# A two-layer decoder trunk in split fp32: a second pair of blocks in seven products in each layer's second FFN, part loads in a list of their own, a new block order

## The chip, the core and the metric

The kernel runs on one core of one Trainium2 chip. The metric is the device time of one execution in microseconds (us). The kernel before takes 984.8 us, the median of three runs (982.86, 984.80, 985.94).

## The reference

A decoder trunk of two layers over 256 tokens of width 1024. Each layer is a half-step SwiGLU FFN, a mixer (layer 0: mLSTM, layer 1: dilated attention, both beside a memory cross-attention), and a second half-step SwiGLU FFN. Between the layers stands a K/V projection. The change concerns the second FFN:

```python
D_MODEL, SEQ, D_FF = 1024, 256, 2816
def swiglu(h, w_gate, w_up, w_down):
    return (jax.nn.silu(h @ w_gate) * (h @ w_up)) @ w_down
...
for layer in range(DEPTH):
    x = x + 0.5 * swiglu(rms_norm(x, ffn1_norm[layer]), ...)
    ...
    x = x + mix
    x = x + 0.5 * swiglu(rms_norm(x, ffn2_norm[layer]), ffn2_w_gate[layer], ffn2_w_up[layer], ffn2_w_down[layer])
```

## The kernel before

**Split fp32.** Every large product is made of three: each operand is split into a high half (`hi`, rounded to the matmul's reduced fp32 format) and the rest (`lo`), and `mm3` (L773) adds x_hi w_lo + x_hi w_hi + x_lo w_hi in PSUM. Weights come from HBM as units of 128 x 1024 (512 KB) into six raw buffers. ScalarE casts a unit to `hi`, VectorE subtracts to get `lo` (`emit_unit`, L631), into a ring of eight `hi` and eight `lo` tiles. Units go through the ring strictly in the order of one list, made by `_stream` (L100); a unit is freed when TensorE has used it.

**The FFN.** The 2816 hidden columns are 11 blocks of 256. For each block and each half of the tokens (t = 0, 1), `gu` (L1061) makes gate and up side by side: 8 chunks of the inner dimension x 3 matmuls of 128x128 by 512 columns, so 48 for a block in four units. `hidden_blocks` (L1026) applies SiLU and the product; `placed` (L1036) turns the result through DRAM (tiles `hb`, `hd`, `ht`) and splits it (`hhb`, `hlb`). `dn` (L1068) makes the down product: 24 matmuls for a block in two units, added in four PSUM banks (`acc`) over all blocks. Block 10 is made at the end, between the last down products.

**Seven products.** In each layer's second FFN one pair of gate/up blocks (5 and 6) is a product of 2x2 quarters (tokens halves by inner halves, inner halves by blocks) and is made with seven products instead of eight (`seventh`, L1130). A product is 4 chunks x 3 = 12 matmuls in two units (k = 0, 2). Its name in a plan is two digits: "45" is product 4 of the pair that begins at block 5. Its activations are differences of quarters, made once per FFN by `sums` (L1102): it adds hi and lo to full tiles `xs`, subtracts quarters (`xd`), and splits the differences (`th`, `tl`). It begins 16 us (layer 0) or 8 us (layer 1) of planned time after the activations are there, and yields 0.5 us after each step. The tiles `xs` lie in the places `pb0` and `pb2`.

Its weights are combinations of quarters, made in three pairs of tiles that are reused in place (`SLOTS`, `remade` L609): a for products 2 and 1, b for 5, 3, 6, c for 4 and 7. Tile a is loaded from quarter 0, b from quarter 3, c from quarter 2 with quarter 0 added by an accumulating DMA from GpSimd's queue. Once product 5's weights are split, VectorE subtracts b from a and GpSimd's queue adds quarter 1 to b; then a is added to b (for 6, once 3 is split) and subtracted from c (for 7, once 4 is split). The results are combined from PSUM on VectorE (`g`, `e`).

**What sets the order.** The program is emitted by a planner: `_Model` (L241) keeps a clock for each engine with a cost for each operation, and chains of steps are emitted when their planned time has come. The order of the blocks is written by hand in `PLANS` (L54): g is gate/up, d is down. Part loads stood in the list of units: `early` (L595) sent one on every third load, from 14 units ahead on, and one pair's parts could be loaded only after the pair before was done (`may_load`, L707). Tile b is loaded only after `sums` (`summed`).

Of the kernel before, what the change touches and what calls it, by code (L numbers as in the profile page):

```python
# [8 lines left out]
F32 = mybir.dt.float32  # L9
# [3 lines left out]
ALU = mybir.AluOpType  # L13
# [40 lines left out]
PLANS = {(1, 2): "g0 g1 g2 d0 g3 d1 g4 d2 25 55 45 35 d3 15 65 d4 75 g7 g8 d5 d6 g9 d7", (0, 2): "g0 g1 g2 d0 g3 d1 g4 25 55 d2 45 35 d3 15 65 d4 75 g7 g8 d5 d6 g9 d7"}  # L54
# [6 lines left out]
EVERY = 3  # L61
# [3 lines left out]

SLOTS = {2: ("a", (0,), None), 5: ("b", (3,), None), 4: ("c", (2, 0), None),
# [174 lines left out]
class _Model:  # L241
# [71 lines left out]
    def product(self, columns, cycles, rows, outs, ins):  # L313
# [9 lines left out]
        self.run("tensor", cycles / (2400 if self.fast else 1200) + 0.0027, outs, ins)  # L323

    def run(self, engine, cost, outs, ins, delay=0.0):
# [8 lines left out]
        for a in outs:  # L334
            self.mark(a, end, True, engine)
        self.latest = max(self.latest, end)


class _Engine:
# [5 lines left out]
    def __getattr__(self, method):  # L345
        call, model, name = getattr(self.engine, method), self.model, self.name

        def traced(out, *args, **kw):
# [8 lines left out]
            if name == "sync" or name == "gpsimd" and method == "dma_start":  # L357
                model.run("sync", max(n * out.partition_size() * 4 / 360e3, 0.06), outs, ins, 2.0)
                return
# [50 lines left out]
class _Kernel:  # L410
    def __init__(self, tc, ctx, io, out, units):
# [18 lines left out]
        self.stored, self.slots, self.made, self.open, self.partp = {}, {}, {}, None, None  # L430
        self.todo, self.turn = [], 0
# [123 lines left out]
    def load_unit(self):  # L555
        i, self.loaded = self.loaded, self.loaded + 1
        if self.units[i][1] is None:
            return
        width = self.units[i][2]
        if self.units[i][1][0] == "parts":  # L560
            self.load_part(i)
            return
# [7 lines left out]
    def load_part(self, i):  # L570
        key = self.units[i][0]
        if self.open != key[1:4]:
            self.begin_parts(key[1:4])
        slot = SLOTS[key[4]][0], key[5]
        while slot not in self.slots:
            self.next_part()
        self.raw[i] = self.slots[slot]

    def begin_parts(self, pair):
        self.open = pair  # L580
        self.slots = {}
        self.todo = [(m, k) for m, k in ((4, 0), (2, 0), (4, 2), (2, 2), (5, 0), (5, 2))]

    def next_part(self):

        m, k = self.todo.pop(0)
        slot, parts, _ = SLOTS[m]
        t = self.work.tile([P, 1024], F32, tag="mem", name="pa") if slot == "a" else \
            self.partp[1].tile([P, 1024], F32, tag=f"p{slot}{k}", name=f"p{slot}{k}")
        self.slots[slot, k] = t  # L590
        self.nc.sync.dma_start(t, self.part_of(self.open + (parts[0], k)))
        for p in parts[1:]:
# [1383 lines left out]
```

## Time and profile before

| | us |
|---|---|
| median of three runs | 984.8 (982.86 to 985.94) |
| span of the profiled execution (first to last instruction) | 981.7 |
| second FFN of layer 0, from its first matmul to the K/V projection's | 319.4 to 499.4 |
| second FFN of layer 1, from its first matmul to the end | 798.3 to 981.7 |

PE is TensorE's matmuls, PEld its weight loads, DVE VectorE, ACT ScalarE, POOL GpSimd, SP SyncE (which issues nearly all DMAs). A row of a group gives the line, engine, operation, what is written and read with shapes, the count, then busy us and mean ns of one, then the idle time before and what ended it. In the chain in order of time a row is start, length, engine, tile, line, count. Most operations are recorded by one helper (L349), so the tile's name tells them apart. A matmul's own duration (about 390 ns) overlaps with its neighbours'; the step from one to the next is what counts. The granted clock of TensorE is 1.000 over the span.

### The profile page before, as it was taken

The numbers are of one execution on the slowest core, as the hardware profiler recorded it, in microseconds if no ns is written. First come the engines' busy times: TensorE is split into PE (matmuls) and PEld (weight loads), VectorE is DVE, ScalarE is ACT, GpSimd is POOL, SyncE is SP. The second block draws the span as 40 slices with busy tenths as digits, with TensorE's granted clock in tenths as the row PEclk, the third lists the DMA queues.
The fourth block names the chain that finished last, engine by engine and source line by source line (L and its number), as shares of the span: only waits on it lengthen the run. The fifth ranks groups of instructions, "written<-read, shape, count | busy, mean of one in ns | idle before, by whom it ended". The sixth has DMA issues, their size and how long they took to land.

```text
span 981.7 us, 13154 instructions
## 1 busy us (share of the span) xinstructions
PE 973.7 (99%) x4655; PEld 809.8 (82%) x4655; DVE 691.0 (70%) x1035; ACT 563.8 (57%) x903; POOL 52.2 (5%) x86
## 2 busy tenths in 40 slices
PE   9999999999999999999999999999999999999998
PEld 6888888899998888888878888888887788878887
DVE  5856656569886787976586677776576679589653
ACT  7656445477565655655466566565564585465541
POOL 0002000010010000000011000000002000000000
PEclk9999999999999999999999999999999999999999
DMA  9968677346355697388657688889627557945751
GB/s 353 321 212 302 212 239 227 112 148 230 118 193 193 202 318 243 116 290 268 235 179 252 226 318 274 336 301 316 246 86 266 207 175 252 375 99 205 272 166 43
DMA packets 85482, 223.95 MB, mean 228 GB/s; under 512 B 8172, under 2 KB 29608, under 8 KB 85416
## 3 DMA queue, kind: packets, MB, share of 16 engines
q1 hardware_dynamic: 84120, 218.88, 64.5%
q0 software_dynamic: 1152, 4.19, 2.3%
q8 instruction: 36, 0.59, 0.3%
q14 instruction: 30, 0.25, 0.1%
q10 hardware_dynamic: 144, 0.04, 0.0%
HBM read 203.66 MB, written 19.42 MB: 227 GB/s over the span
## 4 chain that ended last, share of the span: by engine, by line
PE 95%; DVE 2%; ACT 1%; DMA 1%; issue 1%; SPq 0%; DVEq 0%; ACTq 0%
PE gups L763 47%; PE acc L763 24%; PE aps L763 8%; PE oacc L763 4%; PE kvps L763 3%; PE bqps L763 2%; PE mkvps L763 2%; PE tps L770 1%; DVE s L349 1%; PE po L763 1%; PE tpp L770 1%; PE sc L763 1%; DMA ht<-hd 0%; PE ms L763 0%; PE pn L763 0%
## 5 line engine op out<-in xcount | busy, mean ns | idle before, releaser
L349 DVE TENSOR_TENSOR lo<-raw,hi 128x1024 fp32r<-128x1024 f32 (+2 forms) x263 | 302.7, 1167 | 85.2 <-ACT hi L349 79.7
L349 ACT CAST hi<-raw 128x1024 fp32r<-128x1024 f32 (+2 forms) x263 | 260.1, 1008 | 95.3 <-PE acc L763 40.9
L763 PE MATMUL gups<-lo,xh 128*128 128x512 f32 x656 | 254.9, 391 | 1.6 <-DVE g L349 1.6
L763 PE MATMUL gups<-hi,xh 128*128 128x512 f32 x656 | 254.6, 390 | 0.4 <-ACT hi L349 0.4
L763 PE MATMUL gups<-hi,xl 128*128 128x512 f32 x656 | 254.4, 390 | 0.0
L763 PEld LDWEIGHTS gups<-lo,xh 128*128 128x128 f32 x656 | 123.2, 188 | 27.3 <-DVE g L349 2.1
L763 PEld LDWEIGHTS gups<-hi,xh 128*128 128x128 f32 x656 | 123.3, 188 | 26.4 <-ACT hi L349 1.3
L763 PEld LDWEIGHTS gups<-hi,xl 128*128 128x128 f32 x656 | 123.4, 188 | 26.0
L349 ACT ACTIVATE sil<-gups,rstd 128x256 f32<-128x256 f32 x84 | 39.7, 474 | 146.4 <-PE gups L763 136.3
L763 PE MATMUL acc<-lo,hhb 128*128 128x512 f32 x304 | 119.5, 393 | 0.0
L763 PE MATMUL acc<-hi,hlb 128*128 128x512 f32 x304 | 118.6, 390 | 0.1
L763 PE MATMUL acc<-hi,hhb 128*128 128x512 f32 x304 | 118.3, 389 | 0.0
L349 DVE SCALAR_TENSOR_TENSOR lo<-raw,gains,hi 128x512 fp32r<-128x512 f32 x144 | 99.6, 744 | 16.4 <-ACT hi L349 16.1
L349 DVE SCALAR_TENSOR_TENSOR h<-gups,rstd,sil 128x256 f32<-128x256 f32 x84 | 40.0, 480 | 91.1 <-ACT sil L349 91.0
L349 ACT ACTIVATE hi<-raw,gains 128x512 fp32r<-128x512 f32 x144 | 93.9, 715 | 14.9 <-PE gups L763 5.8
L763 PEld LDWEIGHTS acc<-hi,hlb 128*128 128x128 f32 x304 | 57.1, 188 | 12.4 <-DVE hlb L349 0.5
L763 PEld LDWEIGHTS acc<-lo,hhb 128*128 128x128 f32 x304 | 57.1, 188 | 11.6 <-ACT hhb L349 0.3
L763 PEld LDWEIGHTS acc<-hi,hhb 128*128 128x128 f32 x304 | 57.1, 188 | 11.4
L763 PE MATMUL aps<-lo,xh 128*128 128x384 f32 (+1 forms) x144 | 49.8, 346 | 0.0
L763 PE MATMUL aps<-hi,xl 128*128 128x384 f32 (+1 forms) x144 | 47.5, 330 | 0.0
L763 PE MATMUL aps<-hi,xh 128*128 128x384 f32 (+1 forms) x144 | 47.4, 329 | 0.0
L349 ACT CAST hhb<-ht 128x512 fp32r<-128x512 f32 x38 | 23.5, 619 | 26.4 <-DMA ht<-hd 26.3
(228 smaller groups left out, 1191.2 us busy)
## 6 DMA issues: line engine op xcount, KB each, us to landing
raw<-in_wts SPq DMA_DIRECT2D x294, 512.0 KB, 5.1
raw<-in_wts SPq DMA_DIRECT2D x32, 384.0 KB, 3.8
hd<-hb SPq DMA_DIRECT2D x38, 256.0 KB, 5.6
ht<-hd SPq DMA_DIRECT2D x38, 256.0 KB, 4.6
wo<-hi SPq DMA_DIRECT2D x8, 512.0 KB, 6.7
wo<-lo SPq DMA_DIRECT2D x8, 512.0 KB, 7.3
hi<-wo SPq DMA_DIRECT2D x8, 512.0 KB, 5.5
lo<-wo SPq DMA_DIRECT2D x8, 512.0 KB, 7.2
```

The source lines that it names most:

```text
L349: call(out, *args, **kw)
L763: self.pe.matmul(out, lhsT=lhsT, rhs=rhs, start=start, stop=stop, skip_group_check=more)
L770: self.pe.transpose(out, in_, ident)
```

## The change

Blocks 7 and 8 become a second pair ("27 57 ... 77") in both second FFNs, and both get the same order. The seven activations serve both pairs. A list `todo` of part loads in the order a, b, c for each pair replaces the turn-taking: a part is loaded when its pair's first unit is at most 14 units ahead, when the last product that uses the tile's old content has been split (`LAST`), for b when `summed` is set, and when the planned DMA queue is less than `LEAD` = 3 us ahead. The second pair's tile a has buffers of its own. The planner's cost of a matmul in fp32 at full clock gets 13.3 ns beside its columns instead of 2.7, and accumulating DMAs a cost of their own. The hidden operands `hh`, `hl` of ordinary blocks and some tiles of the mixers move from a shared pool of five buffers to pools of their own (two or four, and four or five buffers).

```diff
-PLANS = {(1, 2): "g0 g1 g2 d0 g3 d1 g4 d2 25 55 45 35 d3 15 65 d4 75 g7 g8 d5 d6 g9 d7", (0, 2): "g0 g1 g2 d0 g3 d1 g4 25 55 d2 45 35 d3 15 65 d4 75 g7 g8 d5 d6 g9 d7"}
+PLANS = {
+    (0, 2): "g0 g1 g2 g3 25 55 d0 d1 d2 45 35 15 65 75 "
+            "d3 g9 g4 27 57 d5 47 37 17 67 77 d4 d9 d6",
+    (1, 2): "g0 g1 g2 g3 25 55 d0 d1 d2 45 35 15 65 75 "
+            "d3 g9 g4 27 57 d5 47 37 17 67 77 d4 d9 d6",
+}
-EVERY = 3
+LEAD = 3.0
 EARLIER = 14
+PARTS = ((2, 0), (2, 2), (5, 0), (5, 2), (4, 0), (4, 2))
+LAST = {"a": (1, 3, 4), "b": (6,), "c": (7,)}
...
-        self.run("tensor", cycles / (2400 if self.fast else 1200) + 0.0027, outs, ins)
+        gap = 0.0133 if self.fast and ins[0].dtype == F32R else 0.0027
+        self.run("tensor", cycles / (2400 if self.fast else 1200) + gap, outs, ins)
...
+    def adding(self, cost, outs, ins):
+
+        start = max([self.clock["sync"]] + [self.ready(a, True, "sync") for a in outs])
+        self.clock["sync"] += cost
+        end = start + cost + 3.0
+        for a in outs:
+            self.mark(a, end, True, "sync")
+        self.latest = max(self.latest, end)
...
+    def begin_parts(self, layer, which, plan, pool):
+
+        self.partp, self.slots = pool, {}
+        self.pairs = [(layer, which, s[1]) for s in plan if s[0] == "st" and s[2] == 2]
+        self.todo = [(p, m, k) for p in range(len(self.pairs)) for m, k in PARTS]
+
+    def before_part(self):
+
+        p, m, k = self.todo[0]
+        slot = SLOTS[m][0]
+        p -= 2 if slot == "a" else 1
+        return [] if p < 0 else [(self.pairs[p], i, k) for i in LAST[slot]]
+
+    def part_ready(self):
+
+        if not self.todo:
+            return False
+        p, m, _ = self.todo[0]
+        if self.index[("st",) + self.pairs[p] + (2, 0)] > self.next + EARLIER:
+            return False
+        if SLOTS[m][0] == "b" and not self.summed:
+            return False
+        chains = [self.made.get(c) for c in self.before_part()]
+        return all(c is not None and c.done for c in chains)
...
     def next_part(self):
 
-        m, k = self.todo.pop(0)
+        p, m, k = self.todo.pop(0)
         slot, parts, _ = SLOTS[m]
-        t = self.work.tile([P, 1024], F32, tag="mem", name="pa") if slot == "a" else \
-            self.partp[1].tile([P, 1024], F32, tag=f"p{slot}{k}", name=f"p{slot}{k}")
...
+        if slot == "a" and p % 2 == 0:
+            t = self.work.tile([P, 1024], F32, tag="mem", name="pa")
+        else:
+            t = self.partp.tile([P, 1024], F32, tag=f"p{slot}{k}", name=f"p{slot}{k}")
...
+        while self.part_ready() and self.model.clock["sync"] < self.now + LEAD:
+            self.next_part()
...
-                hh = self.work.tile([P, FB], F32R, tag="hh", bufs=5, name="hh")
-                hl = self.work.tile([P, FB], F32R, tag="hl", bufs=5, name="hl")
+                hh = fp.tile([P, FB], F32R, tag="hs", bufs=few, name="hh")
+                hl = fp.tile([P, FB], F32R, tag="ls", bufs=few, name="hl")
...
-                    e = self.work.tile([P, 384], F32, tag="hh", bufs=5, name="e")
+                    e = mp.tile([P, 384], F32, tag="hh", bufs=4, name="e")
```

More of the change, by code (lines that the diff above doesn't have):

```diff
@@ L595, in early @@
-    def early(self):
-        for i in range(self.loaded, min(self.next + EARLIER, len(self.units))):
-            key, src = self.units[i][:2]
-            if src and src[0] == "parts" and self.open is None and self.may_load(i):
-                self.begin_parts(key[1:4])
-        self.turn += 1
-        if self.todo and (self.todo[0][0] != 5 or self.summed) and self.turn % EVERY == 0:
-            self.next_part()
+        if slot == "a" and p % 2 == 0:
+            t = self.work.tile([P, 1024], F32, tag="mem", name="pa")
+        else:
+            t = self.partp.tile([P, 1024], F32, tag=f"p{slot}{k}", name=f"p{slot}{k}")
@@ L605, in part_of @@
+        pair = self.pairs[p]
+        self.slots[pair, slot, k] = t
+        self.nc.sync.dma_start(t, self.part_of(pair + (parts[0], k)))
+        for i in parts[1:]:
+            self.nc.gpsimd.dma_start(t, self.part_of(pair + (i, k)), accum_op=ALU.add)
     def part_of(self, part):
@@ L611, in remade @@
         nc = self.nc
-        a, b, c = (self.slots.get((n, k)) for n in "abc")
+        a, b, c = (self.slots.get((pair, n, k)) for n in "abc")
         if m == 5:
@@ L682, in emit_unit @@
             self.load_unit()
+        if src is not None and src[0] == "parts":
+            slot = key[1:4], SLOTS[key[4]][0], key[5]
+            while slot not in self.slots:
+                self.finish(*[self.made[c] for c in self.before_part()])
+                self.next_part()
+            self.raw[i] = self.slots[slot]
         if src is None:
@@ L998, in ffn_in @@
         pairs = (layer, which) in PLANS
+        few = 4 if (layer, which) == (0, 1) else 2
         def activated(ps, t, out, last=False):
@@ L1077, in dn @@
             groups = [(slice(h * 512, (h + 1) * 512), acc[t][h], b == 0, last) for h in range(2)]
-            if (layer, which, t) == (1, 2, 1) and b >= NB - 2:
+            if (layer, which, t) == (1, 2, 1) and b in (left[1], NB - 1):
                 f, a, begins, _ = groups.pop()
@@ L1217, in ffn_in @@
         seven, gain = {}, folded(("gu", layer, which))
+        plan, left = _plan(layer, which)
         self.summed = False
@@ L1222, in ffn_in @@
             chains["sums"] = self.spawn(sums())
-            self.partp = (layer, which), fp
-        plan, left = _plan(layer, which)
+            self.begin_parts(layer, which, plan, fp)
         for step in plan:
```

61 lines of the change are left out of this document (17 added, 44 removed).

## The prediction

> **What bounds the kernel now.** I read the page first (busy shares, then the chain that ended last), then the chain in order of time around both second FFNs, then what TensorE waited for there.
>
> ```profile
> span 981.7 us, 13154 instructions
> PE 973.7 (99%) x4655; PEld 809.8 (82%) x4655; DVE 691.0 (70%) x1035; ACT 563.8 (57%) x903; POOL 52.2 (5%) x86
> ...
> PE 95%; DVE 2%; ACT 1%; DMA 1%; issue 1%; SPq 0%; DVEq 0%; ACTq 0%
> ```
>
> TensorE carries 95% of the chain, so the count of matmuls is the time. How much one costs is read from the chain in order of time, not from the mean duration of a matmul (matmuls overlap):
>
> ```profile
> 319.69 2.09 PE gups L763 x9
> 322.21 26.57 PE gups L763 x117
> ...
> 418.64 24.48 PE gups L763 x108
> 443.12 10.88 PE acc L763 x48
> ...
> 798.53 2.09 PE gups L763 x9
> 801.05 30.63 PE gups L763 x135
> ```
>
> 24.48 us over 108 matmuls and 10.88 over 48 are both 0.2267 us each: 512 columns without a hole. So a gate/up block (48) takes 10.88 us, a down block (24) 5.44, one product of a pair (12) 2.72. The first second FFN (layer 0) begins at 319.4, the other at 798.3. The holes in them are few; what the weight loads of TensorE waited for, and the two matmuls around the longest hole in the timeline:
>
> ```profile
> PEld gups L763 <- DVE g L349: 2.1, 1, 2.1
> PEld acc L763 <- DVE hlb L349: 0.5, 1, 0.5
> PEld acc L763 <- ACT hhb L349: 0.3, 1, 0.3
> ```
>
> ```profile
> 877.54 0.39 PE L763 MATMUL gups<-hi,xl 128*128 128x512 f32 x1
> 879.56 0.50 PE L763 MATMUL gups<-lo,xh 128*128 128x512 f32 x1 [1.64 <-DVE g L349]
> ```
>
> The one hole in layer 1's pair is 2.02 us from start to start, less 0.23 for the matmul in it: 1.8 lost. In layer 0 a down block's operand was late for 0.5 + 0.3 = 0.8.
>
> **The change, part by part.**
>
> *Removed: one product in eight of a second pair, in each layer.* Two ordinary gate/up blocks are 96 matmuls, a pair of seven products is 84. 12 x 0.2267 = 2.72 us per layer, 5.44 in all. Down blocks stay.
>
> *Removed: the two old holes.* Layer 1 ran products 2, 5, 4, 3 without a break, and 3 waited for a chain that begins at 5 (subtract, accumulating DMA, add, split). The new order has three down blocks (16.3 us) between 5 and 4 in the first pair and one (5.44) in the second, as layer 0 had before, where this place had no hole. The first down block now comes after product 5 and not beside the sums of activations, so its operand is in time. Together 1.8 + 0.8 = 2.6 us. What is late next is priced below.
>
> *Added: VectorE and ScalarE work.* A pair splits 14 weight tiles where two blocks split 8, remakes six tiles in place, and makes six combinations from PSUM. The windows of the two stages and of the old pair in layer 0, then the timeline and the groups of layer 0:
>
> ```profile
> core 0: us, PE busy (x) PEld busy (x) DVE busy (x) ACT busy (x) POOL busy (x), PEclk, DMA share, GB/s
> 319.50:499.40 179.90, 179.84 (x803) 148.29 (x802) 135.62 (x172) 101.61 (x138) 5.42 (x8) 1.00 0.71 233
> 798.50:981.70 183.20, 178.22 (x795) 147.20 (x793) 127.71 (x162) 89.97 (x119) 4.41 (x6) 1.00 0.60 204
> ...
> 386.00:421.40 35.40, 35.40 (x158) 29.31 (x157) 34.21 (x39) 22.73 (x26) 0.00 (x0) 1.00 0.47 157
> ```
>
> ```profile
> 400.86 0.68 DVE L349 TENSOR_TENSOR e<-gups,g 128x512 f32<-128x512 f32 x1
> 401.46 2.35 DVE L349 TENSOR_TENSOR lo<-pa,hi 128x1024 fp32r<-128x1024 f32 x2
> 403.73 2.35 DVE L349 TENSOR_TENSOR lo<-pb,hi 128x1024 fp32r<-128x1024 f32 x2
> ```
>
> ```profile
> L349 DVE TENSOR_TENSOR lo<-raw,hi 128x1024 fp32r<-128x1024 f32 x54 | 65.2, 1218 | 15.1 <-ACT hi L349 13.9
> L349 ACT CAST hi<-raw 128x1024 fp32r<-128x1024 f32 x53 | 55.1, 1051 | 18.0 <-PE gups L763 8.5 <-PE acc L763 7.4 <-DMA wo<-hi 1.0
> ```
>
> Queued, a 1024-wide VectorE step follows the last by 1.14 us (2.27 for two) and a 512-wide one by 0.60. Added per layer: 6 splits and 6 remakes at 1.14 and 6 combinations at 0.60, 17.3 us. VectorE was busy for 135.6 of 179.9 us in layer 0 and 127.7 of 183.2 in layer 1, so 153 and 145 of about 177: it still fits. ScalarE gets 6 casts of 1.05, which its 78 idle us of layer 0 cover. What matters is where VectorE's work stands. The old 386 to 421.4 is the old first pair with its three down blocks, 19.0 + 16.3 us of TensorE; VectorE was 34.2 of 35.4 us busy and TensorE had no hole. The new first pair has the same blocks, only with five products in one run at its end. Counted from product 5, VectorE owes 17 splits and 6 remakes (26.2), four combinations (2.4) and about 3.5 of activations and operands before the pair's last weight is due, 32.1 in all; TensorE covers 2.7 + 16.3 + 13.6 less the last 0.7, 31.9. That is level, so I put 1.0 there in layer 0, where VectorE starts with no lead, and 0 in layer 1. The second pairs follow a down block and two gate/up blocks (27.2 us of TensorE for some 19 of VectorE); I put 0.3 each. Bounds for all four pairs: 0, and a hole as in layer 1 before, 1.8 each.
>
> *Moved: the pairs come earlier, behind the sums.* Product 5 reads tiles that share their place with the sums of activations, so its load waits for the last use of those. Before the first pair there now stand four gate/up blocks, 192 matmuls; 41.0 us of them lie behind 322.21 and 801.05 (181 matmuls), so product 2 begins at 363.2 and 842.1 and product 5 at 366.0 and 844.8. In layer 0 that is 22 us earlier than before. The timelines of VectorE and SyncE there, and the landing of part b's loads in layer 0 (362 to 368) and in layer 1 (835 to 846):
>
> ```profile
> 346.80 0.69 DVE L349 TENSOR_TENSOR xd<-xs 128x512 f32<-128x512 f32 x1
> ...
> 348.84 0.65 DVE L349 TENSOR_TENSOR tl<-xd,th 128x512 fp32r<-128x512 f32 x1
> ...
> 362.65 0.68 DVE L349 TENSOR_TENSOR xd<-xs 128x512 f32<-128x512 f32 x1
> ...
> 363.36 0.81 SPq L349 DMA_DIRECT2D pb<-in_wts  x2
> ...
> 816.32 0.68 DVE L349 TENSOR_TENSOR xd<-xs 128x512 f32<-128x512 f32 x1
> ...
> 838.17 1.80 SPq L349 DMA_DIRECT2D pb<-in_wts  x2
> ```
>
> ```profile
> pb<-in_wts SPq DMA_DIRECT2D x2, 512.0 KB, 3.6
> ```
>
> ```profile
> pb<-in_wts SPq DMA_DIRECT2D x2, 512.0 KB, 9.3
> ```
>
> Five differences are taken of the sums. The first took 2.7 us from its start to the end of its low half; with the code's pause of 0.5 that is 3.2 apart if nothing comes between, so the last could end 4 x 3.2 + 0.7 after 346.8, at 360.3; before, among weight splits, it let the load go at 363.36. In the new order fewer splits stand there: weights are split in order, eight ahead at most, and the split of product 5 itself stops those behind it. I take 361.8. The landing took 3.6 in layer 0, with the queue quiet, and 9.3 in layer 1, with other part loads beside it; now loads of part a go early and those of c behind b, so I take 3.6. With the cast (1.05) and the split (1.22) the weights are there at 367.7: a wait of 1.7 us in layer 0. Ends: 0.2, and 363.4 + 9.3 + 2.3 - 366.0 = 9.0. In layer 1 the same count from 816.3 gives 829.8, and even 9.3 + 2.3 behind it is 841.4, ahead of 844.8: 0. Its other end is the old issue, 838.2 + 11.6 - 844.8 = 5.0. Behind a late split everything of ScalarE and VectorE queues that was issued later, the down blocks' weights first; they have 16 us before they are missed.
>
> *DMAs.* Per layer SP issues two loads fewer and GpSimd four accumulating ones more, 1.05 MB in all. The page's list of DMA issues, then the full list's row of the accumulations into b:
>
> ```profile
> hd<-hb SPq DMA_DIRECT2D x38, 256.0 KB, 5.6
> ht<-hd SPq DMA_DIRECT2D x38, 256.0 KB, 4.6
> ```
>
> ```profile
> pb<-in_wts POOLq DMA_DIRECT2D x4, 512.0 KB, 7.1
> ```
>
> Averaged over the stages (the windows above) the queues were 0.71 and 0.60 busy, so the bytes cost nothing. An accumulation (7.1) lies under 19.0 us (three down blocks and product 4) in the first pair and 8.2 plus VectorE's lead in the second; if that lead is gone, about 2 us a pair, inside the bound above. GpSimd has no other work there but the statistics at a stage's start. At the end, product 7 of the last pair needs the way through memory, 5.6 + 4.6, and the operand's split; 21.8 us (three down blocks and half of the last gate/up block) hide it: nothing.
>
> *The planner's clock and buffers.* The planner now counts 226.7 ns for a matmul where it counted 216, which is the pitch measured above. It reorders the emission everywhere, in the mixers too, where most of the 3% of the chain that is VectorE's and ScalarE's lies (29 us). A tenth of it either way, 3 us, is my bound; I take 0. Own buffers for hidden operands and mixer tiles: 0, a wait there would need five live at once.
>
> *Sum.* -5.44 - 2.6 + 1.7 + 1.0 + 4 x 0 + 2 x 0.3 = -4.7. Against the profiled span, 981.7 becomes 977.0. The median of the runs is 984.8, 3.1 above the span, and I leave that alone: 980.1, rounded to **980.0 us**.
>
> **Rivals.** *A: VectorE becomes the bound inside pairs.* Each of four pairs loses what one lost before, 1.8 to 2 us, and the 1.7 in layer 0 stays: 984.8 - 8.0 + 7.6 + 1.7 = 986 at worst, about 984.5 with half of the old holes. For it: 34.2 of 35.4 us busy already, and 17 us more per layer. Against it: that very window had no hole.
>
> *B: slower, by the late part.* If the sums end as before and the load lands as late as in layer 1, product 5 waits 9.0 and 5.0: -8.0 + 14.0 + 1.6 = +7.6, 992.4. It decides from a total wait at product 5 of 9.4 us (8.0 - 1.6 + 3.0). For it: the pair comes 22 us earlier and nothing hurries the sums. Against it: the load queue is emptier then. A long wait may cost more than itself:
>
> ```profile
> 1.25 4.02 PE L1867 MATMUL warm<-warm 128*128 128x512 bf16 x9 [1.25 <-DVE warm L349]
> ```
>
> Out of idleness the first nine matmuls took 0.45 each, twice the pitch; the 2.02 us hole left the next ones at 0.23. If a wait of 9.0 brought that state back for such a 4 us, half of it, 2.0 us, comes on top: 994.4; I give this extra a chance of 0.03 within B. The Trainium skill has it as a rule ("TensorE: Matmul & The Clock Gate", Part 1: an idle window of about 3.4 us halves the clock until a busy window has passed); by it 1.7 us would come on top of every wait above 3.4. The trace agrees at the start and, with 2.02 us, does not reach the limit.
>
> *C: all is covered.* Only the gains stay: 984.8 - 8.0 = 976.8.
>
> **How the numbers follow.** Forecast (978 to 982) 0.48, A 0.25, B 0.13, C 0.14. The range of 8 in 10 reaches from C with a little of the planner's bound, 975.5, to the worst of A, 986.0. What this measurement can tell from no change is about 0.3%, 3 us: faster is below 981.8, slower above 987.8. Faster gets C and nearly all of the forecast, 0.60; same gets A and the forecast's edge, 0.25; slower B and a little of A, 0.15.
>
> **What would show it.** TensorE has 24 matmuls fewer; both FFNs still run at 0.2267. The hole at layer 1's product 3 is gone. In layer 0 a hole of 1 to 3 us stands ahead of product 5, with the load of part b or its cast named as the one waited for. VectorE's busy time rises by about 35 us. I am wrong if the holes in the two FFNs together exceed 8 us, or if the mixers change by more than 3 us.

## The result: slower by 2.2%, and the profile after

The kernel after takes **1005.65 us** (median of four runs, 1004.26 to 1008.73). The kernel before took 983.83 beside it (982.81 to 985.94), so the ratio is 1.0225 (95% interval 1.0202 to 1.0249). The forecast was 980.0, with 986.0 as the upper end. The profiled execution of the new kernel took 1008.73; its span is 1007.0, where 977.0 was expected. So 30.0 us have to be found. That execution is the slowest of the four, 3.1 above their median, so the sizes below are its own and a little large.

First the page of the new kernel: span, busy time, and the chain that ended last by engine.

```profile
span 1007.0 us, 13163 instructions
...
PE 978.6 (97%) x4631; PEld 809.6 (80%) x4631; DVE 725.6 (72%) x1071; ACT 577.8 (57%) x917; POOL 60.7 (6%) x94
...
PE 62%; DMA 15%; DVE 14%; issue 4%; ACT 4%; SPq 0%; POOL 0%; ACTq 0%; DVEq 0%; POOLq 0%
```

The work is what was forecast: 4631 matmuls, 24 fewer, and 34.6 us more of VectorE (35 were expected). What changed is the chain: 15% of it is now DMA (1% before) and 14% VectorE. A third of it now runs through transfers, VectorE and ScalarE, where TensorE carried 95% before.

Where the 30.0 us lie is read from the first matmuls of the stages:

| us | before | forecast | after | off by |
|---|---|---|---|---|
| second FFN, layer 0 | 179.8 | 179.3 | 190.8 | 11.5 |
| second FFN, layer 1, to the end | 183.4 | 179.2 | 189.4 | 10.2 |
| all the rest | 618.5 | 618.5 | 626.8 | 8.3 |

The forecast columns are the prediction's own terms: -2.72 - 0.8 + 1.7 + 1.0 + 0.3 in layer 0, -2.72 - 1.8 + 0.3 in layer 1. The old hole at layer 1's product 3 is gone, as forecast. The rest consists of first FFNs, mixers and the K/V projection, of which the change edits nothing but buffers and the planner's clock.

What TensorE waited for, the two longest entries of the list of waits:

```profile
PE gups L780 <- DVE h L366: 14.2, 4, 6.1
PE gups L780 <- DVE g L366: 1.7, 1, 1.7
```

The columns are total, count and longest, in us. `h` is the product of gate and up of an ordinary block, VectorE's last read of its PSUM bank. Four waits for it make 14.2 us: one ahead of each product 5, in both pairs of both layers. Here is the worst, TensorE's timeline in the second pair of layer 0:

```profile
435.76 0.39 PE L780 MATMUL gups<-hi,xl 128*128 128x512 f32 x1
...
438.48 0.39 PE L780 MATMUL gups<-hi,tl 128*128 128x512 f32 x1
444.92 0.80 PE L780 MATMUL gups<-lo,th 128*128 128x512 f32 x1 [6.05 <-DVE h L366]
445.51 0.63 PE L780 MATMUL gups<-hi,th 128*128 128x512 f32 x1
445.94 0.63 PE L780 MATMUL gups<-hi,tl 128*128 128x512 f32 x1
```

Product 2 ends, and product 5 begins 6.44 us later instead of 0.23: 6.2 lost. Its weights are not late. It needs a bank: gate and up of a block use two banks in turn, product 2 takes the one of t = 0, and product 5 the one of t = 1, which is free only when ScalarE's SiLU and then `h` have read it. The last matmul of that half starts at 435.76 (the first line), so SiLU could run from 436.2. The timelines of ScalarE and of VectorE show when it did:

```profile
440.52 0.62 ACT L366 CAST hhb<-ht 128x512 fp32r<-128x512 f32 x1 [9.26 <-DMA ht<-hd]
441.04 1.99 ACT L366 CAST hi<-raw 128x1024 fp32r<-128x1024 f32 x2
442.93 0.47 ACT L366 ACTIVATE sil<-gups,rstd 128x256 f32<-128x256 f32 x1
```

```profile
433.03 0.68 DVE L366 TENSOR_TENSOR hlb<-ht,hhb 128x512 fp32r<-128x512 f32 x1
...
442.13 2.34 DVE L366 TENSOR_TENSOR lo<-raw,hi 128x1024 fp32r<-128x1024 f32 x2
444.39 0.48 DVE L366 SCALAR_TENSOR_TENSOR h<-gups,rstd,sil 128x256 f32<-128x256 f32 x1
```

ScalarE stood for 9.26 us at `hhb`, the cast of a down block's turned operand, because the transfer that makes `ht` had not landed. Two casts of weights and the SiLU followed it in the queue and ran only after it, and VectorE's splits and `h` after those. SiLU ran 6.8 us after its data were there. And why was `ht` late? SyncE's timeline:

```profile
425.01 9.11 SPq L366 DMA_DIRECT2D ht<-hd  x2
```

These are two loads into the one buffer that `ht` has: the second is issued at 434, since the split of the block before (`hlb` at 433.03 above) had to release the buffer first. That split itself ran 2.2 us after its cast, behind weights of the pair in VectorE's queue.

Layer 1's second pair, ScalarE, then VectorE:

```profile
929.02 0.62 ACT L366 CAST hhb<-ht 128x512 fp32r<-128x512 f32 x1 [5.84 <-DMA ht<-hd]
...
932.75 0.47 ACT L366 ACTIVATE sil<-gups,rstd 128x256 f32<-128x256 f32 x1
```

```profile
933.40 1.22 DVE L366 TENSOR_TENSOR lo<-pc,hi 128x1024 fp32r<-128x1024 f32 x1
934.65 1.23 DVE L366 TENSOR_TENSOR pc<-pc,pa 128x1024 f32<-128x1024 f32 x1
935.79 0.48 DVE L366 SCALAR_TENSOR_TENSOR h<-gups,rstd,sil 128x256 f32<-128x256 f32 x1
```

Such a cast waited 5.84 us here, half a block earlier. The SiLU ended at 933.2, and `h` came 2.6 us later, behind a split and a remaking of the pair's weights.

In the first pairs the same bank is late behind other instructions. Layer 0, ScalarE, then VectorE:

```profile
369.07 1.05 ACT L366 CAST hi<-pb 128x1024 fp32r<-128x1024 f32 x1 [2.28 <-DMA pb<-in_wts]
370.03 0.46 ACT L366 ACTIVATE sil<-gups,rstd 128x256 f32<-128x256 f32 x1
```

```profile
370.16 1.22 DVE L366 TENSOR_TENSOR lo<-pb,hi 128x1024 fp32r<-128x1024 f32 x1 [2.23 <-ACT hi L366]
371.30 1.22 DVE L366 TENSOR_TENSOR pa<-pa,pb 128x1024 f32<-128x1024 f32 x1
372.43 0.48 DVE L366 SCALAR_TENSOR_TENSOR h<-gups,rstd,sil 128x256 f32<-128x256 f32 x1
372.83 1.22 DVE L366 TENSOR_TENSOR lo<-pb,hi 128x1024 fp32r<-128x1024 f32 x1
```

Layer 1, ScalarE, then VectorE:

```profile
861.65 1.05 ACT L366 CAST hi<-pb 128x1024 fp32r<-128x1024 f32 x1 [0.77 <-DMA pb<-in_wts]
862.60 2.00 ACT L366 CAST hi<-raw 128x1024 fp32r<-128x1024 f32 x2
864.50 0.47 ACT L366 ACTIVATE sil<-gups,rstd 128x256 f32<-128x256 f32 x1
```

```profile
863.18 1.22 DVE L366 TENSOR_TENSOR lo<-pb,hi 128x1024 fp32r<-128x1024 f32 x1
864.32 1.22 DVE L366 TENSOR_TENSOR pa<-pa,pb 128x1024 f32<-128x1024 f32 x1
865.46 2.35 DVE L366 TENSOR_TENSOR lo<-raw,hi 128x1024 fp32r<-128x1024 f32 x2
867.73 0.48 DVE L366 SCALAR_TENSOR_TENSOR h<-gups,rstd,sil 128x256 f32<-128x256 f32 x1
```

Part b is loaded late because of the sums, as the prediction said; but its casts also hold the SiLU back, and then the remaking of `pa` holds `h` back. The weights themselves come in two halves (the rows `lo<-pb`). In layer 0 the second was there at 374.05, and without any wait it would have been needed at 372.2: the late weights alone would have lost 1.8. In layer 1 it was there at 864.4, when product 5 could only have begun: there the bank alone was late. Lost ahead of product 5, start to start less 0.23: 2.1 and 6.2 in layer 0, 3.85 and 2.65 in layer 1. Single holes of 0.8 to 1.9 besides (product 7 behind `g` at 403.8, operands of down blocks) bring the holes to about 11.4 and 7.7.

After two of them TensorE also ran slower. The windows from 444 to 456 and from 860 to 875 (columns as in the prediction):

```profile
444.00:456.00 12.00, 11.08 (x37) 8.96 (x38) 11.90 (x14) 7.85 (x10) 0.00 (x0) 0.72 0.44 135
860.00:875.00 15.00, 11.31 (x39) 8.74 (x38) 12.85 (x14) 11.07 (x13) 3.59 (x4) 0.77 0.95 242
```

The granted clock is 0.72 and 0.77 there. Twelve matmuls behind 444.92 follow each other by 0.43 instead of 0.2267: 12 x 0.2 = 2.4 us lost, and as much in layer 1.

Last, the 8.3 us outside. The waits of ScalarE for turned operands, before and then after, show that something has moved everywhere:

```profile
ACT hhb L349 <- DMA ht<-hd: 26.3, 19, 4.2
```

```profile
ACT hhb L366 <- DMA ht<-hd: 58.7, 26, 9.3
```

### The profile page after: what moved, and what is told of

It is laid out like the page before. It is cut to its first block, busy times and chain, and to the rows that moved or that the text cites. A ratio compares the mean times of both kernels' runs of the same rounds, so it can differ in the third digit from the quotient of the medians.

```text
span 1007.0 us, 13163 instructions
## 1 busy us (share of the span) xinstructions
PE 978.6 (97%) x4631; PEld 809.6 (80%) x4631; DVE 725.6 (72%) x1071; ACT 577.8 (57%) x917; POOL 60.7 (6%) x94
## 4 chain that ended last, share of the span: by engine, by line
PE 62%; DMA 15%; DVE 14%; issue 4%; ACT 4%; SPq 0%; POOL 0%; ACTq 0%; DVEq 0%; POOLq 0%
PE gups L780 24%; PE acc L780 17%; DVE lo L366 7%; PE aps L780 6%; DMA hd<-hb 6%; DMA ht<-hd 5%; PE oacc L780 4%; PE kvps L780 3%; PE bqps L780 2%; DMA pb<-in_wts 2%; ACT hi L366 2%; DMA wo<-hi 1%; PE tps L787 1%; DVE h L366 1%; PE mkvps L780 1%
## 5 line engine op out<-in xcount | busy, mean ns | idle before, releaser
L366 DVE TENSOR_TENSOR lo<-raw,hi 128x1024 fp32r<-128x1024 f32 (+3 forms) x247 | 282.9, 1162 | 79.9 <-ACT hi L366 75.2
L366 ACT CAST hi<-raw 128x1024 fp32r<-128x1024 f32 (+3 forms) x247 | 242.8, 1006 | 92.6 <-PE acc L780 33.5
L780 PE MATMUL gups<-hi,xh 128*128 128x512 f32 x608 | 236.3, 391 | 0.7 <-ACT hi L366 0.7
L780 PE MATMUL gups<-lo,xh 128*128 128x512 f32 x608 | 236.6, 392 | 0.0
L780 PE MATMUL gups<-hi,xl 128*128 128x512 f32 x608 | 236.3, 391 | 0.0
L780 PEld LDWEIGHTS gups<-hi,xh 128*128 128x128 f32 x608 | 114.6, 189 | 25.2 <-ACT hi L366 1.6
L780 PEld LDWEIGHTS gups<-hi,xl 128*128 128x128 f32 x608 | 114.7, 189 | 24.0
L780 PEld LDWEIGHTS gups<-lo,xh 128*128 128x128 f32 x608 | 114.6, 188 | 23.6
L780 PEld LDWEIGHTS acc<-hi,hhb 128*128 128x128 f32 x304 | 57.4, 189 | 11.4
L366 ACT CAST hhb<-ht 128x512 fp32r<-128x512 f32 x38 | 23.6, 620 | 58.7 <-DMA ht<-hd 58.7
L366 DVE TENSOR_TENSOR hlb<-ht,hhb 128x512 fp32r<-128x512 f32 x38 | 26.1, 688 | 35.1 <-ACT hhb L366 35.0
L780 PE MATMUL gups<-lo,th 128*128 128x512 f32 x80 | 33.8, 422 | 15.9 <-DVE h L366 14.2
```

The source lines that it names most:

```text
L366: call(out, *args, **kw)
L780: self.pe.matmul(out, lhsT=lhsT, rhs=rhs, start=start, stop=stop, skip_group_check=more)
```

## The experiments

Four theories stood against each other. **Clock**: the planner's truer cost of a matmul emits steps that wait for transfers too early. **Queue**: a step that waits for a DMA stands in ScalarE's queue ahead of the SiLU that frees product 5's bank. **Order**: the new order itself leaves too little between the blocks. **VectorE**: it simply has too much to do in the pairs (the prediction's rival A). Each ratio is against the kernel before on the same chip, with its 95% interval. Sums "outside" and of the FFNs are spans of the stages as in the table above. They come from the one profiled execution of each run, which can lie 3 to 6 us from the run's median (e3, e13, e15), so differences of 1 or 2 us between them prove little.

### e1: the clock alone, in the kernel before

```diff
-        self.run("tensor", cycles / (2400 if self.fast else 1200) + 0.0027, outs, ins)
+        gap = 0.0133 if self.fast and ins[0].dtype == F32R else 0.0027
+        self.run("tensor", cycles / (2400 if self.fast else 1200) + gap, outs, ins)
```

> The kernel before, with one line changed: the planner counts 226.7 ns for a fast matmul instead of 216. Theory 'planner's clock': the 8.4 us that the changed kernel lost outside the two second FFNs (first FFN 2.7, mixers 2.0 and 1.9, the others 1.8) come from this line, so the run takes 990 to 993 us. Rival 'own buffers' (the hidden operands and mixer tiles that moved to pools of their own cause them): the run stays at 984, within 1.5 us.

996.71 us (995.55 to 998.58), ratio 1.0129 (1.0109 to 1.0149): over half of the loss with one number and no second pair. Outside 626.5 (+8.0, as after the whole change), layer 0's second FFN 183.9 (+4.1), layer 1's unchanged. Most of the 4.1 is seen at product 5. ScalarE's timeline before:

```profile
384.28 0.62 ACT L349 CAST hhb<-ht 128x512 fp32r<-128x512 f32 x1
384.80 1.05 ACT L349 CAST hi<-pc 128x1024 fp32r<-128x1024 f32 x1
386.04 0.47 ACT L349 ACTIVATE sil<-gups,rstd 128x256 f32<-128x256 f32 x1 [0.19 <-PE gups L763]
```

and in e1:

```profile
391.24 0.62 ACT L350 CAST hhb<-ht 128x512 fp32r<-128x512 f32 x1 [2.75 <-DMA ht<-hd]
391.77 1.05 ACT L350 CAST hi<-pc 128x1024 fp32r<-128x1024 f32 x1
392.72 0.46 ACT L350 ACTIVATE sil<-gups,rstd 128x256 f32<-128x256 f32 x1
```

The same three instructions. Before, the transfer had landed, and SiLU waited for the matmuls alone. In e1 the cast waits 2.75 us, and TensorE stands 3.33 us from start to start. The old kernel had this place as well, and little room in it: TensorE's and VectorE's timelines there are

```profile
388.56 0.39 PE L763 MATMUL gups<-lo,th 128*128 128x512 f32 x1
```

```profile
387.29 0.48 DVE L349 SCALAR_TENSOR_TENSOR h<-gups,rstd,sil 128x256 f32<-128x256 f32 x1
```

so `h` had released the bank at 387.8, 0.8 us before product 5.

### e2: the whole change with the old clock

```diff
-        gap = 0.0133 if self.fast and ins[0].dtype == F32R else 0.0027
-        self.run("tensor", cycles / (2400 if self.fast else 1200) + gap, outs, ins)
+        self.run("tensor", cycles / (2400 if self.fast else 1200) + 0.0027, outs, ins)
```

> The changed kernel, with that one line put back to 216 ns. Theory 'planner's clock': the stages outside the second FFNs return to their old lengths and the run takes about 997 us; the holes ahead of product 5 stay, since they do not come from it. Rival 'own buffers': 1005, as it was. If the planner's clock also makes the holes in the second FFNs, the run comes near 984 or below it.

1012.74 (1010.54 to 1014.49), ratio 1.0289 (1.0266 to 1.0312). Outside it is back to 619.6, so all but 1.1 of the 8.3 us there are the clock's. But both second FFNs are longer than with the new clock (198.6 and 194.6): there the truer clock helps. The clock can't be the only cause.

### e3: the turned operand's cast emitted 4 us later

```diff
             nc.sync.dma_start(ht, bass.AP(d.tensor, d.offset, [[P, P], [32 * 512, 4], [1, P]]))
-            yield
+            yield 4.0
```

> The changed kernel, with the cast of a turned hidden operand emitted 4 us later in planned time (the pause after its load is 4.0 instead of 0). Theory 'head of the queue': in layer 0's second pair ScalarE stood 9.3 us at such a cast whose load had not landed, the SiLU that frees product 5's PSUM bank stood behind it, and TensorE lost 6.2 us and then 2.7 at half clock; with the cast later these 8.9 go and most of the 2.65 of layer 1's second pair, and the run takes 994 to 998. Rival 'VectorE's throughput' (17 us more VectorE work per layer is what holds TensorE): 1005, within 2.

1002.54 (998.43 to 1007.99), ratio 1.019 (1.0149 to 1.023). ScalarE's wait for `ht` falls from 58.7 to 6.9, and the hole of 6.44 in layer 0's second pair to 2.5; the FFNs win 3.9 and 3.2. The queue theory holds for that hole. Layer 1's second pair keeps one of 3.06, where such a cast still waits 2.48, and the time lies between the two expectations. The profiled run is the fastest of a wide range, so these sizes are rough.

### e4: the new order and clock, with one pair

```diff
-            "d3 g9 g4 27 57 d5 47 37 17 67 77 d4 d9 d6",
+            "d3 g9 g4 g7 d5 g8 d4 d9 d6",
```

> The changed kernel with blocks 7 and 8 as ordinary blocks again in the place of the second pair, one pair in seven products per layer as before, in the new order. Theory 'head of the queue': the holes of the first pairs stay (2.1 + 0.8 in layer 0, 3.85 and 2.7 of half clock in layer 1), those of the second pairs go (6.2 + 2.7 + 1.9 and 2.65), 5.4 us of products come back: about 998. Rival 'VectorE's throughput': with 17 us less for it in each layer no hole is left in the second FFNs, about 990.

1004.81 (999.73 to 1006.89), ratio 1.0201 (1.0161 to 1.024). Without a second pair the time is nearly that of the full change. First-pair holes stay, 4.43 and 3.86 from start to start. The FFNs are 186.5 and 187.3, shorter by 4.3 and 2.1 although 2.72 of products came back in each: the second pair brought 7.0 and 4.8 of losses, and the rest is there without it. So VectorE's load from two pairs can't be what makes the first pairs' holes; for the second pairs this run doesn't decide it.

### e5: a down block between products 2 and 5

```diff
-    (0, 2): "g0 g1 g2 g3 25 55 d0 d1 d2 45 35 15 65 75 "
-            "d3 g9 g4 27 57 d5 47 37 17 67 77 d4 d9 d6",
+    (0, 2): "g0 g1 g2 g3 25 d0 55 d1 d2 45 35 15 65 75 "
+            "d3 g9 g4 27 d5 57 d4 47 37 17 67 77 d9 d6",
```

(and the same for layer 1).

> The changed kernel with another order: a down block stands between products 2 and 5 of each pair (25 d0 55 d1 d2 45 ... and 27 d5 57 d4 47 ...), so that the PSUM bank of the last gate/up block has 8.2 us instead of 2.7 to be freed. Theory 'bank': the four holes ahead of product 5 (2.1, 6.2, 3.85 and 2.65 with twice 2.7 at half clock) shrink by 5.4 us each, all but 1 us of the 20 goes, about 987; where the accumulation into b has only product 4 to cover it in the second pair, 1 to 3 us come back: 987 to 991. Rival 'VectorE's throughput': the holes stay, 1003 to 1006.

1030.7 (1027.78 to 1033.55), ratio 1.0478 (1.0453 to 1.0503), the worst of all. The bank is no longer waited for, but the list of waits has a new head:

```profile
PE acc L780 <- ACT hhb L366: 19.2, 4, 8.5
```

I had moved block 4's down product close behind the block itself, and its way through memory was not done: holes of 5.83 and 8.88. This order was a bad test of the bank; it shows only that the other side of the same resource, the turned operand, is as tight.

### e6 and e8: e1 with landings planned longer, or the cast later

```diff
-                model.run("sync", max(n * out.partition_size() * 4 / 360e3, 0.06), outs, ins, 2.0)
+                model.run("sync", max(n * out.partition_size() * 4 / 360e3, 0.06), outs, ins, 4.0)
```

> The kernel before with the planner at 226.7 ns per matmul and with 4.0 instead of 2.0 us planned for a load or a store to land. Theory 'planned landing': the true clock costs 12 us only because ScalarE then gets casts of turned operands too early against a landing that is planned at 2.7 and takes 4 to 7; with 4.0 the waits of ScalarE on those (60.6 us, 26.3 in the kernel before) fall below 30 and the run comes back to 982 to 987. Rival 'detuned' (any change of the planner's clock spoils an order that was fitted to the old one): 992 or more.

e8 has the edit of e3 in its place:

> The kernel before with the planner at 226.7 ns per matmul and with only the casts of turned hidden operands emitted 4 us later in planned time. Theory 'planned landing': it is these casts that stand at the head of ScalarE's queue, so most of the 12 us goes: 984 to 989. If other waits matter as much (weight loads, the accumulations), 990 to 996.

e6: 999.55 (998.98 to 999.76), ratio 1.016 (1.0145 to 1.0176). Layer 0's first FFN and mixer are back to 199.6 and 119.8, and the wait for `ht` is down to 10.3; outside, 4.3 of the 8.0 are won. The time misses the expected 982 to 987 all the same, for TensorE now waits for operands that come late:

```profile
PE acc L764 <- ACT hhb L350: 8.3, 3, 5.1
```

e8: 993.74 (992.62 to 994.1), ratio 1.01 (1.0085 to 1.0115). Layer 0's hole at product 5 is gone, and ScalarE's wait for `ht` is 9.7. But holes of 2.22 and 1.23 behind late operands take its place, so that layer 0's FFN stays at 184.1, and outside it stays at 624.8. So the cast at the head of the queue explains the hole in the FFN, and not the loss in the mixers: that one reacts to the planned landing of all loads, and only in part.

### e7 and e9: the same two edits in the kernel after

e7 is the kernel after with a planned landing of 4.0, as in e6:

> The changed kernel with 4.0 instead of 2.0 us planned for a load or a store to land. Theory 'planned landing': the 8 us outside the second FFNs and the parts of the holes that come from casts standing at the head of ScalarE's queue go, 985 to 992. Rival 'detuned': 1000 or more.

1000.46 (998.2 to 1002.19), ratio 1.017 (1.0146 to 1.0193). Outside 621.4, 5.4 better than after; holes at the second pairs' product 5 remain, 5.14 and 3.51. e9 is e7 with the edit of e3 on top:

> The changed kernel with 4.0 us planned for a landing and the cast of a turned hidden operand another 4.0 us later in planned time. With the first alone, ScalarE still stood 4.6 us (layer 0) and 2.9 us (layer 1) at such a cast ahead of the SiLU that frees product 5's bank in the second pairs, and TensorE lost 4.9 and 3.3 there. Theory 'head of the queue': both holes go, 990 to 993. Rival: something else holds that SiLU, and the run stays at 1000.

1018.31 (1017.06 to 1020.41), ratio 1.0349 (1.0326 to 1.0372). A miss: both of those holes go, and others come, behind down operands that are cast too late (9.0 for `hhb`, 3.8 for `hlb` in the list of waits); the rest grows to 630.1. Two remedies for the same wait overshoot.

### e10: two buffers for the turned operand

```diff
-            ht = fp.tile([P, 4, P], F32, tag="ht", bufs=1, name="ht")
+            ht = fp.tile([P, 4, P], F32, tag="ht", bufs=2, name="ht")
```

> The changed kernel with two buffers instead of one for the turned hidden operand (ht). In front of the second pair four blocks (5, 6, 9, 4) go through memory one after the other, since the load of the next waits until the one before has been split. Theory 'single buffer': with two, the landings keep pace, the 9.3 us that ScalarE stood in layer 0 shrink to under 4, the hole ahead of product 5 there goes below 3 with no half clock, about 997. Rival: the round trip itself is too long for the plan, and the run stays within 3 us of 1005.

1000.45 (999.92 to 1002.9), ratio 1.017 (1.0148 to 1.0193). The holes at product 5 are gone in both second pairs, with no change of order or clock; those of the first pairs stay, 3.03 and 3.82.

```profile
PE gups L780 <- DVE h L366: 6.1, 2, 3.4
```

Four waits of 14.2 have become two of 6.1. So the single buffer made these holes of the second pairs, and not those of the first. Layer 1's FFN falls to 184.3. Layer 0's falls only to 189.1, for others come there: 2.14 behind `g` (product 7) and 2.51 behind a turned operand, with slower clock behind the latter. And e13 and e16 below show that two buffers are not enough in every order of emission.

### e11 and e12: two more misses

e11 is e9 with another order:

```diff
-    (0, 2): "g0 g1 g2 g3 25 55 d0 d1 d2 45 35 15 65 75 "
-            "d3 g9 g4 27 57 d5 47 37 17 67 77 d4 d9 d6",
+    (0, 2): "g0 g1 g2 g3 25 d0 55 d1 d2 45 35 15 65 75 "
+            "d3 g4 g9 27 d5 57 d6 47 37 17 67 77 d4 d9",
```

> As the kernel with 4.0 us planned for a landing and the later cast, and with one down block between products 2 and 5 of each pair, this time a block whose operand is long ready (25 d0 55 d1 d2 ..., d3 g4 g9 27 d5 57 d6 47 ... 77 d4 d9). Theory 'bank': no hole ahead of product 5 is left, and what remains is VectorE's 1 to 2 us a pair in the run of five products: 986 to 990. Rival 'VectorE's throughput': as many us of holes at other places of the pairs, above 994.

1028.44 (1026.13 to 1032.23), ratio 1.0448 (1.041 to 1.0487). Again no hole at product 5, and late operands instead (17.8 us for `hhb`, six waits). e12 is e2 with the edit of e3:

> The changed kernel with the planner back at 216 ns and the cast of a turned hidden operand 4 us later in planned time. The stages outside the second FFNs are as in the kernel before (they were with the old clock alone). Theory 'head of the queue': of the 30 us of that run's second FFNs the holes ahead of product 5 go (6.0, 5.6, 3.5, with half clock behind each), 990 to 996; if the old clock has its holes elsewhere too, 1000 to 1005.

1006.41 (1005.54 to 1007.96), ratio 1.0228 (1.0207 to 1.0249): layer 1 comes to 184.8, layer 0 stays at 197.0, and the list of waits names VectorE's splits (five waits, 5.1 us) and late operands (7.9). Here VectorE is seen as a limit, in pieces of 1 to 1.4 us.

### e13: e10, and the sums of activations earlier

```diff
-            yield 16.0 if layer == 0 else 8.0
+            yield 6.0 if layer == 0 else 2.0
```

> The changed kernel with two buffers for the turned operand (as in the run with that alone, 1000.5) and with the sums of activations begun 6 and 2 us instead of 16 and 8 us after the activations. Theory 'late part': the holes ahead of product 5 in the first pairs (3.0 and 3.8, each with some half clock) come from the casts of part b, which the sums hold back and behind which the SiLU of the last gate/up block stands; with the sums earlier both go, 989 to 993. Rival: the SiLU stands there for another reason, and the run stays within 3 us of 1000.

998.86 (993.14 to 1001.38), ratio 1.0153 (1.0122 to 1.0183). The first pairs' holes shrink from 3.03 to 0.87 and from 3.82 to nothing: there the late part b was the cause. Holes at the second pairs' product 5 partly return (3.5 and 2.0), although `ht` has two buffers: in layer 0 ScalarE stands 4.33 us at such a cast again. The profiled run is the fastest of a wide range again.

### e14: the order alone, in the kernel before

```diff
+PLANS = {
+    (0, 2): "g0 g1 g2 g3 25 55 d0 d1 d2 45 35 15 65 75 "
+            "d3 g9 g4 27 57 d5 47 37 17 67 77 d4 d9 d6",
+    (1, 2): "g0 g1 g2 g3 25 55 d0 d1 d2 45 35 15 65 75 "
+            "d3 g9 g4 27 57 d5 47 37 17 67 77 d4 d9 d6",
+}
...
-            if (layer, which, t) == (1, 2, 1) and b >= NB - 2:
+            if (layer, which, t) == (1, 2, 1) and b in (left[1], NB - 1):
```

> The kernel before with the new order of blocks and the second pair and nothing else: old part loads within the list of units, the planner at 216 ns, old buffers. Theory 'order': the holes ahead of product 5 belong to the new order (four gate/up blocks without a down block, then two products), so this loses as much as the changed kernel with the old clock, 1005 to 1015. Rival 'load list': the new list of part loads makes them, and this comes near 984.

1024.03 (1022.2 to 1025.28), ratio 1.0399 (1.0374 to 1.0423). The old list of loads, old clock and old buffers, and still 25.7 and 14.3 us more in the two FFNs, with outside 620.1.

```profile
PE gups L768 <- DVE h L354: 20.6, 3, 10.4
```

None of the three waits stands in a first pair: in layer 0 they are ahead of block 4's second half (6.2) and of the second pair's product 5 (3.9), in layer 1 ahead of the second pair's product 2 (10.4). ScalarE's timelines ahead of the last two:

```profile
444.63 0.62 ACT L354 CAST hhb<-ht 128x512 fp32r<-128x512 f32 x1 [10.07 <-DMA ht<-hd]
```

```profile
933.92 0.62 ACT L354 CAST hhb<-ht 128x512 fp32r<-128x512 f32 x1 [10.91 <-DMA ht<-hd]
```

So a loss in the FFNs of this kind needs neither the new list nor the new clock nor the new buffers; the order with its second pair makes it. The rest of the change takes part of it back: 198.6 and 194.6 with the old clock (e2), 190.8 and 189.4 with the new one.

### e15: the new clock in the second FFNs alone

```diff
+        self.paced = False
...
-        gap = 0.0133 if self.fast and ins[0].dtype == F32R else 0.0027
+        gap = 0.0133 if self.fast and self.paced and ins[0].dtype == F32R else 0.0027
...
+            self.model.paced = which == 2
...
+            self.model.paced = False
```

> The changed kernel, with the planner's 226.7 ns only inside the two second FFNs and 216 elsewhere. Theory 'planner's clock': the 8.4 us outside the second FFNs go and those stay as they are, 995 to 999. Rival: the losses of the stages are not separate (what one stage emits early the next pays), and the run stays above 1002.

999.53 (996.13 to 1002.16), ratio 1.0149 (1.0118 to 1.018). Outside 619.9: 6.9 of the 8.3 are back. The 1.4 that stay lie in layer 1's mixer (71.9 for 70.8) and the K/V projection (+0.5). Layer 0's second FFN is shorter too, 185.4 for 190.8, though the planner counts there as before: its hole in the second pair is 3.17 instead of 6.44. So the stages are not quite separate. The profiled run is the fastest of a wide range.

### e16: e10, e13 and e15 together

> The three together: two buffers for the turned operand, earlier sums, the planner's new clock only in the second FFNs. If the three causes are separate, their gains add: 1005.7 less 8.4, less 5, less 9, about 981 to 985, which is the kernel before. If VectorE's throughput is a floor of its own, not below 990.

988.85 (988.0 to 994.11), ratio 1.0054 (1.0033 to 1.0075). That lies between the two expectations. Outside 620.1, the FFNs 185.0 and 182.8; in layer 0 that is hardly less than in the profiles of e13 or e15 (185.4 each), so the gains don't simply add. Holes of 0.9 to 3.2 are left. The longest is at product 5 of layer 0's second pair, and ScalarE's timeline shows the same cause, with two buffers:

```profile
432.32 0.62 ACT L367 CAST hhb<-ht 128x512 fp32r<-128x512 f32 x1 [4.02 <-DMA ht<-hd]
```

### e17 and e18: e16 with other orders

e17 puts down blocks between the products of both pairs:

```diff
-    (0, 2): "g0 g1 g2 g3 25 55 d0 d1 d2 45 35 15 65 75 "
-            "d3 g9 g4 27 57 d5 47 37 17 67 77 d4 d9 d6",
+    (0, 2): "g0 g1 g2 g3 25 d0 55 d1 45 35 15 65 d2 75 "
+            "g9 g4 27 d3 57 d5 47 37 17 67 d4 77 d9 d6",
```

> As the three together (988.9), with a down block whose operand is long ready between products 2 and 5 and before product 7 of both pairs (25 d0 55 d1 45 35 15 65 d2 75, then g9 g4 27 d3 57 d5 47 37 17 67 d4 77 d9 d6). Theory 'bank': the holes ahead of product 5 (1.5, 3.2 and 2.3, with 1.4 of half clock) go, and those ahead of product 7 (0.9, 1.6, 1.7), 10 to 11 us in all, less 1 to 2 for what is late next: 979 to 981, below the kernel before. Rival 'VectorE's throughput': with the down blocks gone from where they gave VectorE its lead, the holes come back elsewhere, 987 or more.

e18 keeps the first pair as it was and changes the second line alone:

```diff
     (0, 2): "g0 g1 g2 g3 25 55 d0 d1 d2 45 35 15 65 75 "
-            "d3 g9 g4 27 57 d5 47 37 17 67 77 d4 d9 d6",
+            "g9 g4 27 d3 57 d5 47 37 17 67 d4 77 d9 d6",
```

> As the three together, with the new places of the down blocks in the second pair alone. Theory 'bank': the second pairs' holes go (3.2 + 1.4 + 1.6 and 2.3 + 1.7), the first pairs' stay: 979 to 982. Rival 'VectorE's throughput': 987 or more.

e17: 999.02 (997.27 to 1003.0), ratio 1.0173 (1.0153 to 1.0194), a miss. There, with fewer down blocks between products 5 and 4 of the first pair, TensorE waits for VectorE's splits of the combined weights (a hole of 2.86 at 383.5), at the last block (10) of layer 0 the transposes wait 4.0 for `h`, and layer 0's FFN is 192.7.

e18: **984.83** (982.66 to 987.44), ratio 1.0014 (1.0003 to 1.0026). That is within the 0.3% that can be told from no change, and the best version with two pairs; none beat the kernel before. It misses the expected 979 to 982, though the second pairs' holes at product 5 did go. The profiled run lies 1.8 above that median. Waits of e18, TensorE:

```profile
PE acc L781 <- ACT hhb L367: 3.2, 2, 2.7
PE po L781 <- ACT mp L367: 1.3, 2, 1.0
PE warm L1887 <- DVE warm L367: 1.2, 1, 1.2
PE gups L781 <- DVE h L367: 1.1, 1, 1.1
```

Of the 14.2 us for `h`, 1.1 is left. Layer 1's FFN takes 179.7, 3.7 less than before, where the prediction had said 4.2 less: with the waits gone the removed work is worth what was counted. Layer 0's takes 185.3, 5.5 more than before. Four holes, the longest of 3.09 at 475.3 behind a turned operand, cost 5.8 there, and the slower clock behind that one 2.0. With 1.4 outside, 5.5 - 3.7 + 1.4 = 3.2 is the difference of the spans (984.9 and 981.7).

## Why the prediction was wrong, point by point

Both of the prediction's own signs of being wrong came: holes of far more than 8 us in the two FFNs, and 3.9 us in the two mixers.

**The products and VectorE: right.** 24 matmuls fewer at 0.2267, and 34.6 us more on VectorE. Layer 1 of e18 shows the gain.

**"It reorders the emission everywhere ... my bound; I take 0": wrong.** The step measured +8.3, beyond its bound of 3 (e1: +8.0 by itself; e2 and e15 take it away). I argued from TensorE's pitch, which the new number meets, and did not ask whether another cost in the planner leans on the old one. The planner lets a load land 2.0 us after its bytes, 2.7 in all for 256 KB, and the lists of DMA issues of both kernels show 4.3 to 5.6. A clock that was 5% too fast for TensorE may have hidden part of that. e6 supports this, since longer planned landings bring back 4.3 of the 8.0; how the clock costs the other part, above all in layer 1's mixer, is open, and e8 shows that the casts of turned operands are not the way.

**"Behind a late split everything of ScalarE and VectorE queues ... they have 16 us before they are missed": wrong**, and this is the step that failed in the FFNs. I named the queue and looked in it for weights of the down blocks. What stands in it as well is the SiLU, which frees product 5's bank, and that is missed after the 2.72 us of product 2. In layer 0 the wait came where the prediction put it and in about its size (2.1 for 1.7): the late weights alone would have made 1.8, and the bank, which the entry names, came as late. In layer 1 it put 0 with 5.0 as the other end. The weights were in time there, and the bank cost 3.85 and 2.4 for the slower clock. The part came late there because the sums end later than I had counted: the load of b stands at 856.2, where 829.8 and the shift of 19.3 make 849.1. e13 shows the part as the cause in both first pairs.

**"I put 0.3 each" for the second pairs: wrong.** They lost 6.2 with 2.4 of slower clock, and 2.65. Their price was taken from VectorE's throughput; the mechanism was a turned operand whose transfer had not landed when its cast stood at the head of ScalarE's queue. In the kernel after, the single buffer of `ht` made it late (e10); with two buffers it can be late again (e13, e16). VectorE's queue has a share in it, before the buffer is free in layer 0 and before `h` in layer 1. The trace of before showed the tight place, `h` 0.8 us ahead of product 5, and a cast for `hhb` two instructions before the SiLU. Priced by the longest wait for such a transfer in the kernel before, 4.2, less this 0.8, my estimate would have been a loss of up to 3.4 at each product 5.

**"ScalarE gets 6 casts of 1.05, which its 78 idle us of layer 0 cover": wrong in kind.** ScalarE was busy for only 57% of the span after, too, but the 9.26 us that it stood at one cast covered nothing: the SiLU behind it ran 6.8 late.

**Own buffers: 0, not shown to be wrong.** With the clock of before outside the second FFNs, 1.1 to 1.6 stays there (e2, e15, e16, e18), 1.1 of it in layer 1's mixer, 71.9 for 70.8. The buffers were not tried by themselves; e14 has the old ones and its mixer takes 71.9 too, which speaks against them.

**The rivals.** A (VectorE) exists as holes of 1 to 2 us, not as the main loss: e4 has one pair and keeps the first pairs' holes, and e10 removes those at the second pairs' product 5 with VectorE's load unchanged. It adds to the other losses where `h` or a split stands in its queue. B (the late part) was there as a cause, but not as B has it: product 5 waited 2.1 and 3.85 instead of 9.0 and 5.0, and in layer 1 for its bank and not for its weights. These 5.95 are below the 9.4 at which B decides; the total over all four pairs, 14.8, is above it only by the turned operands. B's time of 992.4 is missed because two other losses stand beside it. The slower clock behind a long wait, which I gave 0.03, came twice in the kernel after, behind the holes of 6.4 and 4.1, at 2.4 us each. The rule of the Trainium skill ("TensorE: Matmul & The Clock Gate", Part 1: half the clock after an idle window of about 3.4 us) says so of these two, and the trace agrees, with 6.05 and 3.69 us of idleness; I had worked out 1.7 from it.

**Where the gain went.** In e18 the 5.4 us of products are still there, and about 5.8 us of holes and 2.0 of slower clock in layer 0, with 1.4 outside, take them back. No order that was tried covers all three tight places at once: the bank behind the SiLU, the turned operand of a down block, and VectorE's splits between products. Whether one exists is open.

## What to carry to other kernels

Before a product is moved, ask who frees its PSUM bank, and read that engine's queue ahead of the freeing instruction: here one cast that waited 9.26 us for a transfer delayed the SiLU behind it by 6.8 us, on an engine that is busy for 57% of the span. Making one constant of a planner true can cost time (8.0 us outside the FFNs here), perhaps because others were wrong the other way; change it alone first. And where several edits come at once, run each by itself (here e1 and e14): the clock and the order each made a loss without the other. They are not independent, though: the new clock alone cost layer 0's FFN 4.1 us, and in the changed FFNs it saved 7.8 and 5.2 (e2).

## What the runs showed of the hardware

TensorE's slower clock also came behind shorter holes than I expected. Behind holes of 3.33 (e1), 3.22 (e16), 3.09 (e18), 2.82 (e17) and once of 2.20 us (e9), from start to start, five to ten matmuls ran at about 0.43 each; behind 2.88 in the kernel after and 2.02 in the one before none did. The page of the Trainium skill named above has about 3.4 us; here, with a matmul of 0.39 in each hole, it happened at 1.8 to 2.9 us of idleness, and the length of the hole alone does not decide it. Each such stretch cost 1.0 to 2.0 us on top of the hole.

Several kernels with new clock and buffers spread by 6 to 10 us from run to run (e3, e4, e13), where the kernel before spreads by 2 to 5; what differs between those runs was not found.
